# A decoder layer on one core: bank copies behind the splits, attention's output with three pairs, and two turns moved

## The chip, the cores and the metric

The kernel runs on one core of a Trainium2 chip. The metric is the device time of one execution in microseconds (us), here as the median of several runs. The engines are TensorE (PE, matmuls), VectorE (DVE), ScalarE (ACT), GpSimd (POOL) and SyncE (SP, which here only issues transfers).

## The reference

One layer of a hybrid decoder with 256 tokens of width 2048, all in float32. Two mixers work side by side on the normalised input: a gated linear recurrence, and attention with 16 heads of 128 in stick-breaking form. Their outputs are gated and merged, then projected; a gated feed-forward network and a gate with a per-layer input follow.

```python
h = rmsnorm(x, g_mix)
x_r, g_r, q, k, v, gate_r, gate_a = split(h @ w_in)
y_r = (gelu(g_r) * rg_lru(conv1d(x_r))) @ w_rnn_out            # "ro"
o   = stick_breaking_attention(head_rmsnorm(q), head_rmsnorm(k), v)   # "qk", "v"
y_a = o @ w_attn_out                                            # "ao"
x   = x + (sigmoid(gate_r) * y_r + sigmoid(gate_a) * y_a) @ w_o # "wo"
g, u = split(rmsnorm(x, g_ffn) @ w_ffn_gu)                      # "gu"
x   = x + (silu(g) * u) @ w_ffn_down                            # "dn"
x   = x + sigmoid(rmsnorm(x, g_ple) @ w_ple_gate) * (p @ w_ple_proj)  # "pg"
```

The names behind the lines are those that the kernel gives to its stages.

## The kernel before

**Three products for one.** Every matmul operand is a float32 number, held as a high part and the low rest, both in a rounded type (fp32r). A product of two is the sum of three matmuls, each 128 x 128 by 128 x 512: high by high (L657), high by low (L658), low by high (L659), in `prod`. Each weight chunk of 128 x 1024 is therefore *split* before use: ACT copies it to the high part (L374), DVE subtracts that from the weight to get the low part (L375).

**Fewer products by sums.** Most stages are computed in groups (`group`), each of 256 tokens by 1024 columns of output, in a scheme with seven products of blocks where the plain way has eight. For some *pairs* of 128-row steps of the weights, sums of weight blocks are formed (DVE L296, and a few by accumulating transfers that POOL issues, L334), and sums of the activations (`half_sums`). A group's list of *slots* names the order: whole numbers are plain steps (four products each), "11", "21", "22", "T1" to "T4" and ("S", i, p) are steps on sums. Pairs 0, 1 make the first part; ("S", i, 2) is a third pair, ("S", i, 3) a fourth. Lists with three pairs are `FIRST3` and `EVEN3`, 61 products; with four pairs `EVEN4`, 60 products. `FOUR` names the stages with four.

**Banks.** A group collects its products in PSUM banks named "B", "5", "2", "3", "4" and "8". When the partial sums "11", "T1", "T2", "T3" are complete, ACT copies the bank to SBUF (the *bank copies*, `actv(t, ps, AF.Copy)`, L460 in the profile); after T3, DVE makes two differences of the copies. The results then are four *joins*, a bank plus a copy, on DVE (L454).

**What is issued when.** The instructions of one engine run in their order in its queue. A scheduler sets this order at build, from the order of the program and estimated times. `tc.issue_after(ins)` puts what is issued inside it behind the instruction `ins` on its engine. Weights are streamed by `Stream`: it loads, sums and splits up to four chunks ahead of the matmul that asks for one, and remembers its last splits in `hi_ins` and `lo_ins`. Work that can wait is put on a list with a due time (`later_on`), and issued by `run_todo` at the slots of the next group once its time has come, each behind the last splits (`behind_splits`). The four joins are due at `JOINS_AT`, 0, 1.3, 2.7 and 4.0 us into the next group. While such work is left on the list, the turned rows (transposes, `next_mix`) that the next stage needs are held back.

**Attention.** The heads are worked in eight pairs `hp` between the blocks of matmuls for the last Q and K columns and for the gate: `step` is called before every slot of those blocks, and each slot has a list of attention steps: `att_t` (transposes of a head pair's rows, PE L1021), `att_z` (scores), `att_e` (masks and exponents) and `att_o` (the product with V). `TURN_AT` gives the slot of `att_t`, `ATT_FROM` and `ATT_AT` those of the others. From slot 60 on, the sums of attention's output for the stage "ao" are made (`parts_sums`). A slot holds four products, twelve matmuls.

**Around the change.** The order of stages is: ... gate blocks with attention, ao (two groups), wo (two), the feed-forward network (gu, dn), pg (two). `whole` computes a group and lists its joins. After each ao group, every result is joined, multiplied by its gate and added to the other mixer's result (`join`, due at 2.7 + 1.36 i); these rows are then turned for wo.

Of the kernel before, what the change touches and what calls it, by code (L numbers as in the profile page):

```python
# [10 lines left out]
AF = mybir.ActivationFunctionType  # L11
ALU = mybir.AluOpType
# [22 lines left out]
FIRST3 = ["11", A1, 6, "T1", A2, 7, "T2", "21", "22", A3, "T3", 8, A4, 9, "T4", 10, 11, 12, 13, 14, 15]  # L35
EVEN3 = ["11", A1, 6, "T1", A2, 7, "21", 8, "T2", 9, "22", A3, 10, "T3", 11, A4, 12, "T4", 13, 14, 15]
# [3 lines left out]
TWELVE = [("S", 1, 0), ("S", 1, 1), 4, ("S", 2, 0), 5, ("S", 2, 1), 6, ("S", 3, 0), 7, ("S", 3, 1), 8, ("S", 4, 0), 9,  # L40
          ("S", 4, 1), 10, 11]
TWO = (0, 1)
FOUR = ("gu", "v", "ro", "qk", "ao")
LAST_GROUP = ("pg", 1)
W_BUFS = 4
RAW_AHEAD = 12.0
# [37 lines left out]

ATT_AT = (2, 7, 11)
ATT_FROM = (-1, 6, 14, 21, 29, 36, 43, 51)
TURN_AT = (None, None, 8, 12, 25, 30, 42, 49)


def rg_k_tiles(j):  # L90
# [77 lines left out]
def tail():  # L168


    def wide(name, w, slots, c=0):
        return [(name, g, w, c + 8 * g, c + 8 * g + 4, slots[g]) for g in range(2)]

    def blocks(*cs):
        return [("blk", b, None, c, None, None) for c, b in cs]

    def gu(*gs):
        return [("gu", g, "gu", 4 * g, 44 + 4 * g, EVEN4 if g else FIRST3) for g in gs]

    def dn(q):  # L180
        k, p = FQ0[q], FQ0[q] // 2
        slots = [x + k if isinstance(x, int) else (*x[:2], x[2] + p) if isinstance(x, tuple) else x
                 for x in (EVEN3 if FQ[q] == 16 else TWELVE)]
        return wide(f"dn{q}", "dn", [slots] * 2)

    x = [("x", 0), ("x", 1)]
    return (wide("ro", "ro", [LONG] * 2) + wide("v", "in", [EVEN4] * 2, C_V)
            + [("qk", b, "in", C_Q + 4 * b, C_K + 4 * b, EVEN4) for b in range(2)]
            + blocks(*[(c, b) for b in (2, 3) for c in (C_Q, C_K)], *[(C_GTA, b) for b in range(4)])
            + wide("ao", "ao", [EVEN4] * 2) + wide("wo", "wo", [FIRST3, EVEN3]) + gu(0, 1, 2, 3) + dn(0) + gu(4, 5, 6, 7) + dn(1)  # L190
            + gu(8, 9, 10) + dn(2)
            + wide("pg", "pg", [FIRST3[:-4] + x + FIRST3[-4:]] * 2))

# [233 lines left out]
def tile_hybrid_block(ctx: ExitStack, tc: tile.TileContext, xT: bass.AP, x: bass.AP, pT: bass.AP,  # L427
# [25 lines left out]
    def tt(o, a, b, op):  # L453
        nc.vector.tensor_tensor(o, a, b, op)  # L454
# [4 lines left out]
    def actv(o, i, f, **kw):  # L459
        nc.scalar.activation(o, i, f, **kw)  # L460
# [176 lines left out]

    pend, todo = [], []

    def later_on(at, f, first=True):  # L640

        todo.append((at, f, first))

    def run_todo(t):
        due = [x for x in todo if x[0] <= t]
        todo[:] = [x for x in todo if x[0] > t]
        for _, f, _ in due:
            with behind_splits():
                f()

    def tok(pairs, k, t):
# [69 lines left out]
    def group(at, pairs, sums, after=None, also=()):  # L721

        name, g = at
        slots = [x for n, y, _, _, _, sl in HEAD + TAIL if (n, y) == at for x in sl
                 if isinstance(x, int) or is_sum(x)]  # L730
        turned_at = TURNED_AT["twelve" if len(slots) == len(TWELVE) else
                              "first" if slots[2] == 6 and slots[8] == "22" else "even"]
        seq = [(n, q, 0, 512) for n, x in enumerate(slots) for q in products(x, pairs_of(name)[:2])]
        if at == LAST_GROUP:
            k = len(slots) - 4
            rest = [q for q in seq if q[0] >= k]
            seq = [q for q in seq if q[0] < k] + [q for b in "243" for q in rest if q[1][0] == b]
            seq += [(n, (b + f, *q), e, e + 256) for e, f in ((0, "a"), (256, "b")) for n, (b, *q), _, _ in rest
                    if b == "8"]
        first, last = {}, {}  # L740
        for i, (_, (b, y, _, _), e, _) in enumerate(seq):
            first.setdefault(b, i)
            last[b, e] = i
            if y in ("11", "T1", "T2", "T3"):
                last[y] = i
        banks, tile_, got = {}, {}, {}
        begin = [0.0]
        for x in slots:
            begin.append(begin[-1] + 0.68 * len(products(x)))
        turns = list(turned_at)  # L750
        for i, (n, (b, y, p, c), e0, e1) in enumerate(seq):
            if n not in got:
                if n in also:
                    also[n]()
                run_todo(begin[n])
                if pend and turns and n >= turns[0] and not any(x[2] for x in todo):
                    turns.pop(0)
                    with tc.issue_after(mm_.ins):
                        pend.pop(0)()
                got[n] = S_.take(("tok", name, g, slots[n]))  # L760
            if b not in banks:
                banks[b] = psum()
            ps = banks[b]
            if p is None:
                o = tok(pairs, *y)
            else:
                o = {"11": tok(pairs, 2 * p, 0), "21": tok(pairs, 2 * p + 1, 0), "22": sums[p][3],
                     "T1": sums[p][0], "T2": sums[p][1], "T3": sums[p][2],
                     "T4": tok(pairs, 2 * p + 1, 1)}[y]
            _, _, hi, lo, w0 = got[n].columns(c)  # L770
            s = slice(w0 + e0, w0 + e1)
            mm_ = prod(ps[:, e0:e1], o, hi[:, s], lo[:, s], i == first[b], i in (last[b, e0], last.get(y)),
                 b == "B")
            if y in ("11", "T1", "T2", "T3") and i == last[y]:
                t = tile_[y] = tl("T")
                actv(t, ps, AF.Copy)
                if y == "T3":
                    tt(tile_["T2"], tile_["T1"], tile_["T2"], ALU.subtract)
                    tt(tile_["T1"], tile_["T1"], t, ALU.subtract)
                    if after is not None:  # L780
                        after(tile_)
        tile_["ends"] = [banks[b] for b in ("8a", "8b") if b in banks]
        return [banks[b] for b in "2438"], tile_

# [104 lines left out]
    @contextmanager  # L889
    def behind_splits():  # L890
        with tc.issue_after(S_.hi_ins.ins), tc.issue_after(S_.lo_ins.ins):
            yield
# [52 lines left out]
        else:  # L945
            pend_gtr = pss

    def whole(at, pairs, sums, also=()):

        qs_, t = group(at, pairs, sums, None, also)  # L950
        cs = [t[y] for y in ("11", "T3", "T2", "T1")]
        for a, c, q in zip(JOINS_AT, cs, qs_):
            later_on(a, (lambda c, q: lambda: tt(c, q, c, ALU.add))(c, q))
        return cs

    def parts_sums(pairs, sums, p):
        h = tl("T")
        hi, lo = parts(pairs[p])
        tt(pair(h), f32(hi), f32(lo), ALU.add)
        sums[p] = half_sums(h)  # L960
# [150 lines left out]
            at.setdefault(ATT_FROM[hp] + f, []).append(((att_z, att_e, att_o)[d], hp))  # L1111
    osum = {}
    for i, p in enumerate(pairs_of("ao")):
        at.setdefault(60 + i, []).append((lambda p: parts_sums(ost, osum, p), p))
    slot = [0]

    def step():
# [42 lines left out]
        return run  # L1160

    for g in range(2):
        for i, o in enumerate(whole(("ao", g), ost, osum)):
            def join(o=o, c=gta[2 * g + i // 2][i % 2], m=mix_r[2 * g + i // 2][i % 2]):
                tt(c, o, c, ALU.mult)
                tt(c, c, m, ALU.add)

            later_on(2.7 + 1.36 * i, join)
        pend.extend(next_mix(p) for p in range(4 * g, 4 * g + 4))

    x1 = [[None] * 4 for _ in range(2)]
# [72 lines left out]
    def gu(g):  # L1244
        also = {13: lambda: token_scales(0, rs1)} if g == 0 else {}
        c11, c21, c12, c22 = whole(("gu", g), hg, hsum, also)
        def gated(c, s_, t):
            def run():
                actv(s_, s_, AF.Silu, scale=rs1[:, t:t + 1])
                stt(c, c, rs1[:, t:t + 1], s_, ALU.mult, ALU.mult)  # L1250
            return run

        later_on(5.4, gated(c12, c11, 0))
        later_on(8.1, gated(c22, c21, 1))

        def turn(f):
            def run():
                ps = psum()
                for e in range(2):
                    for t, a in enumerate((c12, c22)):  # L1260
                        c = (2 * f + e) * P
                        o = e * 256 + t * P
                        nc.tensor.transpose(ps[:, o:o + P], a[:, c:c + P], ident)  # L1263
                p = 2 * g + f
                if p in summed:
                    h = tl("T")
                    actv(h, ps, AF.Copy)
                    acts[p] = split(h, "A")
                    asum[p] = half_sums(h)
                else:  # L1270
                    acts[p] = split(ps, "A")
            return run

        pend.extend(turn(f) for f in range(2))
# [120 lines left out]
```

## Time and profile before

| | us |
|---|---|
| median of 3 runs | 1856.26 |
| lowest and highest | 1856.01, 1857.22 |
| the profiled execution | 1855.46 |
| its span in the trace | 1853.8 |

The page gives one profiled execution: the busy time of each engine, the chain of work that ended last, and groups of instructions by line. An engine's busy time, set beside the span, says how much room it has; whether another engine's work matters is told by the waits on the engine that has none. Line numbers are those of the kernel before. Some matmul records can be missing, and the ends of matmuls are modelled: two matmuls that follow each other overlap in the rows.

### The profile page before, as it was taken

To read this page: it belongs to the slowest core of one execution; us is meant where nothing else is said; L and a number is where in the kernel's file an instruction comes from. 1 tells how busy PE (TensorE), PEld (TensorE's weight loads), DVE (VectorE), ACT (ScalarE), POOL (GpSimd) and SP (SyncE) were. 2 spreads that over 40 slices of the span, in tenths; PEclk is the share of its full clock that TensorE was granted. 3 is DMA by queue.
4 is the path that set the end of the run, shared out by engine and by line. 5 is a ranking of instruction groups with operands and counts; after the bars stand their busy time and mean duration, and the time that the engine had idled before them with its cause. 6 is when DMAs were issued, how large, how long until landed. Compare 5 with 4: busy or idle time off the path is not lost.

```text
span 1853.8 us, 24812 instructions
## 1 busy us (share of the span) xinstructions
PE 1839.0 (99%) x8849; PEld 1546.0 (83%) x8849; DVE 1542.4 (83%) x1954; ACT 1275.8 (69%) x1710; POOL 133.1 (7%) x160
## 2 busy tenths in 40 slices
PE   9999999999999999999999999999999999999998
PEld 7899889888888888888877888888888888888787
DVE  7688888677899977667899889888799988898886
ACT  7687888775566767776665687665576655676675
POOL 0000000011011100000110001100111101111000
PEclk9999999999999999999999999999999999999999
DMA  8555555588788854446988788887888878887774
GB/s 296 175 177 187 184 197 198 197 251 259 240 252 238 255 174 159 151 157 219 257 234 241 223 256 240 246 246 246 254 261 253 234 235 251 251 251 235 210 242 133
DMA packets 123964, 415.42 MB, mean 224 GB/s; under 512 B 13888, under 2 KB 14528, under 8 KB 123840
## 3 DMA queue, kind: packets, MB, share of 16 engines
q1 hardware_dynamic: 101808, 359.82, 54.8%
q0 software_dynamic: 21888, 54.01, 17.2%
q8 instruction: 69, 1.13, 0.2%
q14 instruction: 55, 0.45, 0.1%
q10 hardware_dynamic: 144, 0.01, 0.0%
HBM read 411.69 MB, written 2.10 MB: 223 GB/s over the span
## 4 chain that ended last, share of the span: by engine, by line
PE 97%; DVE 2%; ACT 1%; issue 0%; DMA 0%; SPq 0%; DVEq 0%; ACTq 0%
PE ps L657 26%; PE ps L659 26%; PE ps L658 26%; PE ps L576 9%; PE ps L580 5%; PE ps L559 1%; PE ps L560 1%; PE ps L558 1%; DVE wlo L375 1%; DVE H L454 1%; PE ps L1263 1%; PE ps L1208 0%; PE ps L1021 0%; DMA H<-in_x_dram 0%; DVE Q L454 0%
## 5 line engine op out<-in xcount | busy, mean ns | idle before, releaser
L658 PE MATMUL ps<-wlo,Q 128*128 128x512 f32 x2173 | 846.7, 390 | 0.5 <-DVE wlo L375 0.5
L659 PE MATMUL ps<-whi,Q 128*128 128x512 f32 x2173 | 843.2, 389 | 2.6 <-DVE Q L454 2.6
L657 PE MATMUL ps<-whi,Q 128*128 128x512 f32 x2173 | 752.3, 392 | 4.0 <-ACT whi L374 2.2
L375 DVE TENSOR_TENSOR wlo<-w,whi 128x1024 fp32r<-128x1024 f32 (+2 forms) x474 | 570.5, 1208 | 163.4 <-ACT whi L374 159.1
L374 ACT ACTIVATE whi<-w 128x1024 fp32r<-128x1024 f32 (+2 forms) x474 | 493.8, 1048 | 216.9 <-PE ps L659 166.3
L374 ACT ACTIVATE whi<-Q 128x1024 fp32r<-128x1024 f32 (+1 forms) x385 | 384.8, 1005 | 212.4 <-PE ps L659 177.9
L375 DVE TENSOR_TENSOR wlo<-Q,whi 128x1024 fp32r<-128x1024 f32 (+1 forms) x385 | 441.5, 1155 | 61.8 <-ACT whi L374 58.0
L657 PEld LDWEIGHTS ps<-whi,Q 128*128 128x128 f32 x2173 | 407.5, 188 | 89.2 <-ACT whi L374 3.3
L659 PEld LDWEIGHTS ps<-whi,Q 128*128 128x128 f32 x2173 | 408.0, 188 | 87.2 <-DVE Q L454 2.8
L658 PEld LDWEIGHTS ps<-wlo,Q 128*128 128x128 f32 x2173 | 408.3, 188 | 83.7 <-DVE wlo L375 1.5
L334 POOL DMA_DIRECT2D Q<-in_w_dram x152 | 130.6, 866 | 1669.9 <-PE ps L659 623.1
L576 PE MATMUL ps<-Q,whi 128*128 128x512 f32 x704 | 170.7, 392 | 0.0
L576 PEld LDWEIGHTS ps<-Q,whi 128*128 128x128 f32 x704 | 128.8, 188 | 24.5
L296 DVE TENSOR_TENSOR Q<-Q,Q 128x512 f32<-128x512 f32 (+1 forms) x152 | 130.6, 877 | 15.1 <-DMA Q<-in_w_dram 14.7
L460 ACT ACTIVATE H<-ps 128x512 f32<-128x512 f32 (+1 forms) x179 | 94.2, 540 | 61.1 <-PE ps L659 51.0
L454 DVE TENSOR_TENSOR H<-H,H 128x512 f32<-128x512 f32 (+1 forms) x216 | 121.0, 571 | 4.9 <-ACT H L460 4.3
L454 DVE TENSOR_TENSOR H<-ps,H 128x512 f32<-128x512 f32 (+1 forms) x162 | 97.2, 610 | 9.5 <-PE ps L659 5.1
L580 PEld LDWEIGHTS ps<-Q,wlo 128*128 128x128 f32 x704 | 90.4, 191 | 3.5
L580 PE MATMUL ps<-Q,wlo 128*128 128x256 f32 x704 | 91.5, 283 | 0.0
L460 ACT ACTIVATE Q<-H 128x512 fp32r<-128x512 f32 x71 | 43.8, 626 | 37.5 <-DVE H L454 36.9
L460 ACT ACT_TABLE_LOAD x52 | 66.7, 1283 | 3.1 <-DVE Q L454 2.2
L454 DVE TENSOR_TENSOR Q<-H,Q 128x512 fp32r<-128x512 f32 (+1 forms) x79 | 53.9, 688 | 3.0 <-ACT Q L460 2.9
(125 smaller groups left out, 898.6 us busy)
## 6 DMA issues: line engine op xcount, KB each, us to landing
w<-in_w_dram SPq DMA_DIRECT2D x449, 512.0 KB, 4.3
Q<-in_w_dram SPq DMA_DIRECT2D x206, 512.0 KB, 6.0
Q<-in_w_dram POOLq DMA_DIRECT2D x54, 512.0 KB, 7.0
Q<-in_w_dram POOLq DMA_DIRECT2D x98, 256.0 KB, 5.1
w<-in_w_dram SPq DMA_DIRECT2D x16, 448.0 KB, 3.2
H<-in_x_dram SPq DMA_DIRECT2D x8, 256.0 KB, 6.3
H<-in_xT_dram SPq DMA_DIRECT2D x7, 256.0 KB, 5.7
out_dram<-H SPq DMA_DIRECT2D x7, 256.0 KB, 2.5
```

The source lines that it names most:

```text
L296: add = lambda o, a, b: self.nc.vector.tensor_tensor(o, a, b, ALU.add)
L334: self.nc.gpsimd.dma_start(t[:, c:], src[:, a:a + 1024 - c], accum_op=ALU.add)
L374: self.hi_ins = self.nc.scalar.activation(h[:, q], t[:, q], AF.Copy)
L375: self.lo_ins = self.nc.vector.tensor_tensor(l[:, q], t[:, q], h[:, q].bitcast(F32), ALU.subtract)
L454: nc.vector.tensor_tensor(o, a, b, op)
L460: nc.scalar.activation(o, i, f, **kw)
L558: nc.tensor.matmul(o, wt[0], xh, start=start, stop=False)
L576: nc.tensor.matmul(pss[e], wt[0], rhs(xs, k), start=(k == 0), stop=(k == n - 1))
L580: nc.tensor.matmul(pss[e][:, :256], wt[1], rhs(xs, k)[:, :256], start=False, stop=False)
L657: nc.tensor.matmul(ps, x[0], wh, start=start, stop=False, skip_group_check=goes_on)
L658: nc.tensor.matmul(ps, x[0], wl, start=False, stop=False, skip_group_check=goes_on)
L659: return nc.tensor.matmul(ps, x[1], wh, start=False, stop=stop, skip_group_check=goes_on)
```

## The change

There are four parts.

- In `group`, the bank copies on ACT are issued behind the latest high split, and the two differences after T3, and what a stage hangs on them (`after`), behind the latest low split.
- Stage "ao" leaves `FOUR`, and its two groups use `EVEN3` in place of `EVEN4`. The sums for its three pairs are made in slots 61 to 63; before, those for four pairs in slots 60 to 63.
- In "ao", `whole(..., tied=False)` makes the four joins due at once, at 0, and `join`'s gate operations at 1.36 i in place of 2.7 + 1.36 i. Neither is put behind the splits.
- `TURN_AT` moves the turn of head pair 2 (heads 4 and 5) from slot 8 to slot 10, and that of pair 4 from 25 to 26.

```diff
-FOUR = ("gu", "v", "ro", "qk", "ao")
+FOUR = ("gu", "v", "ro", "qk")
...
-TURN_AT = (None, None, 8, 12, 25, 30, 42, 49)
+TURN_AT = (None, None, 10, 12, 26, 30, 42, 49)
...
-            + wide("ao", "ao", [EVEN4] * 2) + wide("wo", "wo", [FIRST3, EVEN3]) + ...
+            + wide("ao", "ao", [EVEN3] * 2) + wide("wo", "wo", [FIRST3, EVEN3]) + ...
...
-    def later_on(at, f, first=True):
+    def later_on(at, f, first=True, tied=True):
...
-        todo.append((at, f, first))
+        todo.append((at, f, first, tied))
...
-        for _, f, _ in due:
-            with behind_splits():
+        for _, f, _, tied in due:
+            with behind_splits() if tied else nullcontext():
                 f()
...
                 t = tile_[y] = tl("T")
-                actv(t, ps, AF.Copy)
+                with tc.issue_after(S_.hi_ins.ins):
+                    actv(t, ps, AF.Copy)
                 if y == "T3":
-                    tt(tile_["T2"], tile_["T1"], tile_["T2"], ALU.subtract)
-                    tt(tile_["T1"], tile_["T1"], t, ALU.subtract)
-                    if after is not None:
-                        after(tile_)
+                    with tc.issue_after(S_.lo_ins.ins):
+                        tt(tile_["T2"], tile_["T1"], tile_["T2"], ALU.subtract)
+                        tt(tile_["T1"], tile_["T1"], t, ALU.subtract)
+                        if after is not None:
+                            after(tile_)
...
-    def whole(at, pairs, sums, also=()):
+    def whole(at, pairs, sums, also=(), tied=True):
...
-            later_on(a, (lambda c, q: lambda: tt(c, q, c, ALU.add))(c, q))
+            later_on(a if tied else 0.0, (lambda c, q: lambda: tt(c, q, c, ALU.add))(c, q), True, tied)
...
-        at.setdefault(60 + i, []).append((lambda p: parts_sums(ost, osum, p), p))
+        at.setdefault(61 + i, []).append((lambda p: parts_sums(ost, osum, p), p))
...
-        for i, o in enumerate(whole(("ao", g), ost, osum)):
+        for i, o in enumerate(whole(("ao", g), ost, osum, tied=False)):
...
-            later_on(2.7 + 1.36 * i, join)
+            later_on(1.36 * i, join, True, False)
```

More of the change, by code (lines that the diff above doesn't have):

```diff
@@ L189, in tail @@
             + blocks(*[(c, b) for b in (2, 3) for c in (C_Q, C_K)], *[(C_GTA, b) for b in range(4)])
-            + wide("ao", "ao", [EVEN4] * 2) + wide("wo", "wo", [FIRST3, EVEN3]) + gu(0, 1, 2, 3) + dn(0) + gu(4, 5, 6, 7) + dn(1)
+            + wide("ao", "ao", [EVEN3] * 2) + wide("wo", "wo", [FIRST3, EVEN3]) + gu(0, 1, 2, 3) + dn(0) + gu(4, 5, 6, 7) + dn(1)
             + gu(8, 9, 10) + dn(2)
```

## The prediction

> **What bounds the kernel now.** I read the head of the page first, then who waited on TensorE, then the table by stretches, and only then single moments. The page:
>
> ```profile
> span 1853.8 us, 24812 instructions
> PE 1839.0 (99%) x8849; PEld 1546.0 (83%) x8849; DVE 1542.4 (83%) x1954; ACT 1275.8 (69%) x1710; POOL 133.1 (7%) x160
> PE 97%; DVE 2%; ACT 1%; issue 0%; DMA 0%; SPq 0%; DVEq 0%; ACTq 0%
> ```
>
> TensorE (PE) is busy for 1839.0 of 1853.8 us, and the chain that ended last runs through it for 97%. Work taken from VectorE (DVE), ScalarE (ACT) or the DMA queues is therefore worth only what PE waits for them. All of these waits (engine line, waited for: us, times, longest) are:
>
> ```profile
> PE ps L659 <- DVE Q L454: 2.6, 1, 2.6
> PE ps L657 <- ACT whi L374: 2.2, 3, 1.1
> PE ps L495 <- DVE H L492: 1.6, 1, 1.6
> PE ps L657 <- DVE Q L454: 1.2, 1, 1.2
> PE ps L657 <- DVE H L454: 0.5, 1, 0.5
> PE ps L658 <- DVE wlo L375: 0.5, 1, 0.5
> ```
>
> That is 8.6 us; the 1.6 of L495 lies at the kernel's start, which the change does not touch, and 7.0 are left. The table by stretches (us; busy time and count of PE, PEld, DVE, ACT, POOL; granted clock, DMA share, GB/s) says where:
>
> ```profile
> 700.00:960.00 260.00, 260.00 (x1270) 219.09 (x1269) 200.90 (x279) 183.89 (x282) 10.33 (x12) 1.00 0.61 195
> 960.00:1000.00 40.00, 35.13 (x156) 26.98 (x155) 39.23 (x48) 22.74 (x27) 3.44 (x4) 1.00 0.75 204
> 1000.00:1750.00 750.00, 750.00 (x3374) 620.44 (x3373) 657.05 (x760) 490.72 (x591) 78.97 (x92) 1.00 0.81 246
> 1750.00:1760.00 10.00, 8.94 (x39) 6.84 (x38) 7.55 (x10) 4.62 (x6) 2.59 (x3) 1.00 0.69 137
> 1760.00:1848.00 88.00, 87.69 (x406) 72.91 (x404) 69.75 (x84) 61.00 (x84) 4.33 (x5) 1.00 0.61 192
> ```
>
> Three places hold nearly all of it: the 1.2 us on L454, near 696 (attention's heads 4 and 5, turned), 4.87 in 960 to 1000 (the start of wo0, the output projection's first group), 1.06 in 1750 to 1760 (the start of pg0). Between them PE never waits, at full clock, so an edit there can win nothing and can only open a new wait.
>
> PE's own price comes from the chain:
>
> ```profile
> 71.41 3.65 PE ps L576 x16
> ```
>
> 3.65 / 16 = 0.228 us from one 512-column matmul to the next.
>
> **What a stop costs.** First the turned heads:
>
> ```profile
> 694.67 1.04 PE L1021 MATMUL ps<-ident,H 128*128 128x128 f32 x8
> 696.15 1.01 DVE L454 TENSOR_TENSOR Q<-Q,ps 128x512 f32<-128x512 f32 x2
> 696.88 0.50 PE L657 MATMUL ps<-whi,Q 128*128 128x512 f32 x1 [1.17 <-DVE Q L454]
> ```
>
> A matmul row lasts 0.39 but the next one normally starts after 0.228, so a stop loses its idle time and that overlap of 0.16; and the first matmul after it takes 0.50 instead of 0.39, 0.11 more. A stop costs its idle plus about 0.27: here 1.17 + 0.27 = 1.44.
>
> **Heads 4 and 5 turned two steps later (-1.44).** Now eight transposes, the previous heads' mask work and a new block's first matmul meet in slot 8. That matmul needs a PSUM bank, and the bank handed to it is the one that the DVE subtraction at 696.15 still reads. With the turn in slot 10, the block of K begins in slot 8 on banks that the score step left earlier, and by slot 10, two slots of twelve matmuls (2.7 us each) later, the bank in question is free. The turned heads' score step comes in slot 16, six slots later, so nothing else becomes late; the same move from 25 to 26 meets no wait now and keeps three slots of room. I take the whole 1.44; at worst the stop moves and nothing is won.
>
> **The start of wo0 (-6.6).** These rows, of ACT, DVE and PE, follow each other:
>
> ```profile
> 964.72 1.83 DVE L296 TENSOR_TENSOR Q<-Q,Q 128x1024 f32<-128x1024 f32 x2
> 966.68 0.60 ACT L460 ACTIVATE H<-ps 128x512 f32<-128x512 f32 x1 [4.90 <-PE ps L659]
> 967.17 1.06 ACT L374 ACTIVATE whi<-Q 128x1024 fp32r<-128x1024 f32 x1
> 967.31 0.69 DVE L454 TENSOR_TENSOR H<-H,H 128x512 f32<-128x512 f32 x1 [0.77 <-ACT H L460]
> 967.92 0.69 DVE L296 TENSOR_TENSOR Q<-Q,Q 128x512 f32<-128x512 f32 x1
> 968.70 1.06 ACT L374 ACTIVATE whi<-Q 128x1024 fp32r<-128x1024 f32 x1 [0.47 <-DVE Q L296]
> 969.81 1.08 PE L657 MATMUL ps<-whi,Q 128*128 128x512 f32 x2 [1.13 <-ACT whi L374]
> 973.12 1.22 DVE L375 TENSOR_TENSOR wlo<-w,whi 128x1024 fp32r<-128x1024 f32 x1
> 973.26 0.50 PE L657 MATMUL ps<-whi,Q 128*128 128x512 f32 x1 [0.53 <-DVE H L454]
> 974.25 0.69 DVE L454 TENSOR_TENSOR H<-ps,H 128x512 f32<-128x512 f32 x1
> 980.12 1.23 DVE L375 TENSOR_TENSOR wlo<-Q,whi 128x1024 fp32r<-128x1024 f32 x1
> 981.41 0.50 PE L658 MATMUL ps<-wlo,Q 128*128 128x512 f32 x1 [0.47 <-DVE wlo L375]
> 991.15 1.30 DVE L454 TENSOR_TENSOR Q<-ps,Q 128x512 fp32r<-128x512 f32 x2
> 991.90 1.20 PE L659 MATMUL ps<-whi,Q 128*128 128x512 f32 x4 [2.60 <-DVE Q L454]
> ```
>
> Four stops: 1.13 + 0.53 + 0.47 + 2.60 = 4.73, plus 4 x 0.27 = 5.8. The row at 969.81 holds two matmuls over 1.08, so their starts are 0.58 apart instead of 0.23: 0.35 more, and 0.11 for the second; a like small stop near 983 brings the sum to 6.6.
>
> A count agrees. The same 40 us held, among 156 instructions of PE, 16 transposes:
>
> ```profile
> L1151 PE MATMUL ps<-ident,Q 128*128 128x128 f32 x16 | 2.5, 276 | 0.0
> ```
>
> A transpose takes PE 0.11 ((1.04 - 0.27) / 7 from the row at 694.67): 140 x 0.228 + 16 x 0.11 = 33.7, which leaves 6.3.
>
> The first two stops come from the order on ACT. It idles 4.90 us in front of the copy of bank "11", while the sum that it could split was ready when the first L296 of 964.72 ended, near 965.95. DVE then waits 0.77 for the same copy before it can make the next sum. Behind the split of plain slot 7 the copy lets the T1 split start 1.2 us sooner, and the sum of 967.92 follows directly at 966.55, done by 967.2; its split ends at 968.3, when PE wants it (968.5). The bank of 973.26 is freed by a join that ran late; untied joins begin as soon as their banks end.
>
> The last two stops come from DVE, 39.23 of 40 us busy: 4 joins and 8 gate operations lie among the splits as late as 988, and the mixed rows are turned and subtracted, at 991.15, just when PE needs them. I walk the new order. DVE's pitch is 0.60 for a join or half-width sum and 1.13 for a split or full-width sum (973.12, 974.25 and on). From the first join to the low split of T2 stand 12 x 0.60, four low splits and one wide sum (5 x 1.13) and one sum of 0.60: 13.5 us. The first bank ends nine matmuls (2.05 us) before attention's output ends, so that split ends 11.5 to 12.2 us after that end. PE reaches it after 48 matmuls (10.9), eight transposes (0.9) and one more matmul (0.2): 12.0. So DVE is what is late next, by nothing or by 0.2; I book one stop of 0.4. Later low splits come every 1.13 where PE needs one per 1.37, so it does not grow, and the turned rows' sums end four us before their transposes.
>
> **Three pairs in attention's output (+1.4).** Each of two groups computes 61 products instead of 60, three matmuls each: 6 x 0.228 = 1.37 on PE, which has no cover. What it saves per group, one and a half wide splits on each of ACT and DVE and two sums, about 2.9 us of DVE, is worth nothing inside the stage (no waits in 700 to 960); it is what lets DVE reach wo0 without arrears, and it is in the walk.
>
> The Trainium skill, TensorE: Matmul & The Clock Gate, section Back-to-back issue gap, gives about 131 ns sustained for a 512-wide matmul; an estimate by it would be 0.8 us instead of 1.37. The trace's 228 ns decides here.
>
> **The start of pg0 (-1.6).**
>
> ```profile
> 1750.69 1.73 POOL L334 DMA_DIRECT2D Q<-in_w_dram  x2 [28.39 <-DVE Q L296]
> 1752.43 0.60 ACT L460 ACTIVATE H<-ps 128x512 f32<-128x512 f32 x1 [4.92 <-PE ps L659]
> 1755.49 0.50 PE L657 MATMUL ps<-whi,Q 128*128 128x512 f32 x1 [0.61 <-ACT whi L374]
> 1756.44 0.96 PE L657 MATMUL ps<-whi,Q 128*128 128x512 f32 x3 [0.45 <-ACT whi L374]
> 1760.67 0.40 PE L657 MATMUL ps<-whi,Q 128*128 128x512 f32 x1
> ```
>
> The same copy, the same cure: 0.61 + 0.45 + 2 x 0.27 = 1.6. ACT stood idle 4.92 us ahead of it, and the splits can go into that. The page of the profile gives for the transfers of the first row's kind (KB each, us from issue to landing):
>
> ```profile
> Q<-in_w_dram POOLq DMA_DIRECT2D x98, 256.0 KB, 5.1
> ```
>
> The one for T2's sum, issued at 1750.69, is what is late next: 1750.69 + 5.1, a sum of 1.13 and a split of 1.06 give 1758.0, and PE's first matmul on T2, now at 1760.67, moves up to 1759.1. The stop is gone, with a microsecond to spare.
>
> **Costed at nothing.** Bank copies in the other groups: each now waits behind one more high split, 1.06. PE writes the same bank again after 18 matmuls, 4.1 us, in the tightest list, so a copy of 0.60 behind a split of 1.06 stays 2.4 us clear. T1 and T2 subtractions and the x1 additions wait behind one low split, 1.22; they feed additions that are needed only at the next stage. On SyncE's queue the loads of x1 move ahead of some wo0 weights as their slots come free earlier, but the weight load in front of them waits longer still. POOL issues four accumulating loads fewer. After the last matmul nothing changes.
>
> **Sum.** -1.44 - 6.6 - 1.6 = -9.65; +1.37 for six matmuls; +0.4 for DVE: -7.9. The profiled execution took 1855.46 (its span and 1.66 around it), so 1847.6; the median of the runs, 1856.26, lies 0.80 above it, and I set the forecast at 1856.26 - 7.9 = 1848.4. About 0.2%, 3.7 us, is what a measurement of this kernel tells from no change.
>
> **Rivals.**
> - DVE remains the limit of wo0. It has 39.23 us of work where PE, without stops, spends 33.7; taking off the 2.9 saved and the 0.77 it idled leaves 1.9 over, and 4.8 if the saving is lost earlier to waits. Then 1848.4 - 0.4 + 1.9 to 4.8 = 1849.9 to 1852.8. For it: the margins above are a few tenths. Against: splits and sums for later slots need not all be done by 1000. Chance 0.18.
> - The order hardly changes where it matters: the copies go late but a sum or a join keeps the splits waiting as before, and only the turn and part of the rest is won: between 1853 and 1856.26 + 1.4 = 1857.7. Against: ACT's 4.90 and 4.92 us of idle time are named as waits for that bank. Chance 0.10.
> - Slower: the copies of all 29 groups go behind splits that themselves wait for a sum or a load, and the bank is not free when PE comes back. It decides once such a split starts more than 2.4 us after the bank is done. A stop then costs 0.27 and its wait; two in each group with no wait to speak of are 58 x 0.27 = 15.7, and the time 1864. For it: every bank copy now inherits the split's wait. Against: ACT is at 69% and mostly splits ahead of need. Chance 0.06.
>
> **How the numbers follow.** All three stalls go: 0.66, from 1847.4 (no stop left, a small gain unseen) to 1849.7. With DVE's case 0.84 lies below 1852.8. The range 1847.0 to 1853.0 takes both, and leaves out the third and fourth. Faster by over 0.2% is below 1852.55: the first case and nearly all of the second, 0.82. Within it: the third with a rest, 0.11. Slower: 0.07.
>
> **What would show it.** In the changed profile: no idle time near 696 and near 1755; in the wo0 stage the high split of T1 directly behind its sum, with the "11" copy after slot 7's split; all joins within four us of attention's output's end; six more matmuls. DVE near 100% for ten us there with a PE wait on L375 or L454 above one us would be the second case. PE waits on ACT L460 or DVE L454 spread over groups that have none now would make me wrong.

## The result and the profile after

Over 20 runs each the changed kernel takes 1853.24 us (1851.61 to 1854.43), the kernel before 1856.48 (1855.23 to 1857.96). The ratio is 0.9982, 95% interval 0.9975 to 0.9989: 3.2 us faster, where 7.9 were forecast. It lies just above the range, and just inside the 0.2% that I had called no change. The profiled execution took 1853.38 with a span of 1851.7.

Line numbers behind 640 are up by one from the kernel before (the three matmuls are now L658 to L660), those behind 780 by up to three. The waits of PE after (us, times, longest):

```profile
PE ps L658 <- DVE H L454: 2.1, 1, 2.1
PE ps L495 <- DVE H L492: 1.6, 1, 1.6
PE ps L658 <- ACT whi L374: 1.4, 2, 1.0
PE ps L659 <- DVE wlo L375: 0.5, 1, 0.5
```

The waits of the kernel before, but that of L495 at the start, are gone from their places. Those on this list stand elsewhere: 2.1 and 0.5 us in pg0, 1.0 of L374 in gu0 and its other 0.4 at the kernel's start. The table by stretches shows the stages:

```profile
690.00:700.00 10.00, 10.00 (x53) 8.52 (x53) 8.36 (x12) 5.25 (x7) 0.00 (x0) 1.00 0.63 206
960.00:1000.00 40.00, 40.00 (x185) 32.88 (x184) 37.97 (x46) 23.07 (x28) 2.98 (x4) 1.00 0.78 231
1040.00:1060.00 20.00, 18.97 (x84) 15.36 (x83) 18.09 (x27) 8.63 (x11) 2.59 (x3) 1.00 0.73 200
1740.00:1765.00 25.00, 22.33 (x94) 17.70 (x93) 22.30 (x28) 17.66 (x27) 3.44 (x4) 0.93 0.71 166
```

The turned heads and wo0 are as forecast, without a stop (156 instructions of PE in 960 to 1000 before, 185 now). But gu0 stops where it did not before, and pg0 stops longer. The last row's clock of 0.93 was 1.00 before. PE's rows there:

```profile
1745.68 0.50 PE L659 MATMUL ps<-wlo,Q 128*128 128x512 f32 x1 [0.55 <-DVE wlo L375]
...
1750.12 0.39 PE L660 MATMUL ps<-whi,Q 128*128 128x512 f32 x1
1752.63 0.50 PE L658 MATMUL ps<-whi,Q 128*128 128x512 f32 x1 [2.12 <-DVE H L454]
1752.97 0.40 PE L659 MATMUL ps<-wlo,Q 128*128 128x512 f32 x1
1753.20 0.49 PE L660 MATMUL ps<-whi,Q 128*128 128x512 f32 x1
1753.49 2.33 PE L658 MATMUL ps<-whi,Q 128*128 128x512 f32 x5
```

After the stop, five matmuls take 2.33 us. Taking off the last one's 0.63, four steps of 0.43 are left, where 0.228 is usual: PE runs at about half its clock for some 3 us. The granted clock is 0.50 from 1753.36 to 1756.77, which is 3.41 us.

How one stage stands is told below by its *lost time*: the sum, over its matmuls, of what the distance from one start to the next exceeds the usual one for that shape, from the trace of one execution of each kernel, good to about 0.1. Between 0.1 and 0.5 in a stage is the usual rest around transposes.

Each ratio is to runs of the kernel before on the same chip, whose median was 1856.5 to 1856.8.

| kernel | median us | ratio to before, 95% interval | turned heads | wo0 | gu0 | pg0 |
|---|---|---|---|---|---|---|
| before | 1856.5 | | 1.46 | 6.98 | 0.35 | 1.95 |
| after | 1853.24 | 0.9982 (0.9975 to 0.9989) | 0.12 | 0.52 | 1.66 | 5.16 |
| e2_no_lo | 1847.23 | 0.9949 (0.9936 to 0.9961) | 0.12 | 0.44 | 0.36 | 0.35 |
| e2b_no_copies | 1855.83 | 0.9996 (0.9988 to 1.0005) | 0.12 | 0.52 | 6.33 | 3.30 |
| e3_part1_only | 1857.34 | 1.0005 (0.9997 to 1.0014) | 1.40 | 4.87 | 1.67 | 3.57 |
| e4_turn_only | 1855.92 | 0.9996 (0.9987 to 1.0005) | 0.12 | 8.61 | 0.36 | 1.95 |
| e1_no_order | 1848.47 | 0.9956 (0.9944 to 0.9969) | 0.12 | 0.44 | 0.36 | 1.95 |
| e6_lo_not_dn | 1848.95 | 0.9960 (0.9947 to 0.9972) | 0.12 | 0.51 | 1.66 | 0.35 |
| e7_earlier_split | 1846.70 | 0.9947 (0.9934 to 0.9959) | no waits of PE behind the kernel's start, in any stage | | | |
| e8_four_pairs | 1852.51 | 0.9977 (0.9967 to 0.9987) | 0.12 | 6.71 | 0.36 | 0.35 |
| e9_late_joins | 1848.15 | 0.9957 (0.9944 to 0.9971) | 0.12 | 1.72 | 0.36 | 0.35 |

### The profile page after: what moved, and what is told of

The parts are those of the page before. It is cut to its first block, busy times and chain, and to the rows that moved or that the text cites. A ratio compares the mean times of both kernels' runs of the same rounds, so it can differ in the third digit from the quotient of the medians.

```text
span 1851.7 us, 24795 instructions
## 1 busy us (share of the span) xinstructions
PE 1840.0 (99%) x8855; PEld 1547.8 (84%) x8855; DVE 1535.5 (83%) x1940; ACT 1269.9 (69%) x1705; POOL 129.5 (7%) x156
## 4 chain that ended last, share of the span: by engine, by line
PE 96%; DVE 2%; ACT 1%; DMA 1%; issue 0%; SPq 0%; ACTq 0%
PE ps L658 26%; PE ps L659 26%; PE ps L660 26%; PE ps L576 9%; PE ps L580 5%; PE ps L559 1%; PE ps L560 1%; PE ps L558 1%; DVE wlo L375 1%; DVE H L454 1%; DMA w<-in_w_dram 1%; PE ps L1266 1%; PE ps L1024 0%; ACT whi L374 0%; PE ps L1211 0%
## 5 line engine op out<-in xcount | busy, mean ns | idle before, releaser
L660 PE MATMUL ps<-whi,Q 128*128 128x512 f32 x2175 | 845.4, 389 | 0.0
L658 PE MATMUL ps<-whi,Q 128*128 128x512 f32 x2175 | 752.4, 392 | 3.5 <-DVE H L454 2.1
L374 ACT ACTIVATE whi<-w 128x1024 fp32r<-128x1024 f32 (+2 forms) x478 | 497.6, 1047 | 215.5 <-PE ps L660 167.3
L374 ACT ACTIVATE whi<-Q 128x1024 fp32r<-128x1024 f32 (+1 forms) x377 | 376.5, 1004 | 227.9 <-PE ps L660 182.1
L375 DVE TENSOR_TENSOR wlo<-Q,whi 128x1024 fp32r<-128x1024 f32 (+1 forms) x377 | 431.3, 1153 | 66.7 <-ACT whi L374 64.1
L658 PEld LDWEIGHTS ps<-whi,Q 128*128 128x128 f32 x2175 | 408.6, 188 | 88.0 <-DVE H L454 2.5
L660 PEld LDWEIGHTS ps<-whi,Q 128*128 128x128 f32 x2175 | 408.6, 188 | 84.3
L334 POOL DMA_DIRECT2D Q<-in_w_dram x148 | 126.8, 863 | 1671.6 <-PE ps L660 670.3
L454 DVE TENSOR_TENSOR H<-H,H 128x512 f32<-128x512 f32 (+2 forms) x214 | 119.3, 570 | 2.2 <-ACT H L460 1.0
L454 DVE TENSOR_TENSOR H<-ps,H 128x512 f32<-128x512 f32 (+1 forms) x162 | 96.6, 606 | 11.5 <-PE ps L660 6.9
L454 DVE TENSOR_TENSOR Q<-H,Q 128x512 fp32r<-128x512 f32 (+1 forms) x78 | 52.9, 683 | 2.1 <-ACT Q L460 2.1
```

The lines of the kernel that those rows point to most:

```text
L334: self.nc.gpsimd.dma_start(t[:, c:], src[:, a:a + 1024 - c], accum_op=ALU.add)
L374: self.hi_ins = self.nc.scalar.activation(h[:, q], t[:, q], AF.Copy)
L375: self.lo_ins = self.nc.vector.tensor_tensor(l[:, q], t[:, q], h[:, q].bitcast(F32), ALU.subtract)
L658: nc.tensor.matmul(ps, x[0], wh, start=start, stop=False, skip_group_check=goes_on)
L660: return nc.tensor.matmul(ps, x[1], wh, start=False, stop=stop, skip_group_check=goes_on)
```

## The experiments

**Where the loss comes from: the low-split part, the copies, or the lead.** The first part of the change has two halves: the bank copies on ACT behind the high split, and the DVE work after T3 (two differences, and in wo and dn the additions to x1) behind the low split. Each was undone by itself, the first part was put alone on the kernel before, and so were the turns.

```diff
e2_no_lo, against after
-                    with tc.issue_after(S_.lo_ins.ins):
-                        tt(tile_["T2"], tile_["T1"], tile_["T2"], ALU.subtract)
+                    tt(tile_["T2"], tile_["T1"], tile_["T2"], ALU.subtract)
...
e2b_no_copies, against after
-                with tc.issue_after(S_.hi_ins.ins):
-                    actv(t, ps, AF.Copy)
+                actv(t, ps, AF.Copy)
...
e3_part1_only, against before
+                with tc.issue_after(S_.hi_ins.ins):
+                    actv(t, ps, AF.Copy)
...
+                    with tc.issue_after(S_.lo_ins.ins):
+                        tt(tile_["T2"], tile_["T1"], tile_["T2"], ALU.subtract)
...
e4_turn_only, against before
-TURN_AT = (None, None, 8, 12, 25, 30, 42, 49)
+TURN_AT = (None, None, 10, 12, 26, 30, 42, 49)
```

> The changed kernel, with the T1 and T2 differences and the x1 additions after T3 issued as before, not behind the latest low split; all else of the change stays. Theory A (these DVE instructions, moved, make the turned rows of pg0 late, and that is where the gain went): the stops of pg0 fall from about 5.2 us of lost time to between 0.4 and 2, the clock stays at 1.00 there, the time is 1848.5 to 1850. Theory B (the bank copies behind the high split do it): no change, 1853. Theory C (PE, 5 us earlier after wo0, catches up with ACT and DVE at pg0 whatever their order): no change, 1853.

1847.23 us: theory A, and 1.3 us below the range that it gave. The only wait of PE left in the whole kernel is the one at its start:

```profile
PE ps L495 <- DVE H L492: 1.6, 1, 1.6
```

and the stretch of pg0 is full, at full clock:

```profile
1740.00:1765.00 25.00, 25.00 (x118) 20.69 (x117) 24.59 (x31) 19.87 (x34) 3.44 (x4) 1.00 0.67 140
```

B and C fall: the copies are as in the changed kernel, and PE comes to pg0 still earlier.

> The changed kernel, with the bank copies on ACT issued as before, not behind the latest high split; the differences and x1 additions stay behind the low split. Theory A: pg0 keeps its stops or gets 1.6 us more, and wo0's first stops come back in part: 1853 to 1857. Theory B: pg0's stops go, 1850 or below. Theory C: 1853 to 1856.

1855.83, inside A's range, but inside C's too, and the stages are only in part as A had them: pg0 keeps stops (3.30), wo0's first stops do not come back (0.52), and gu0 loses 6.33, which no theory had. The clock has a share in that. PE stops five times between 1053.4 and 1060.7, for 0.95, 0.30, 0.68, 0.78 and 0.45 us, and then the stretch reads:

```profile
1060.00:1064.00 4.00, 3.55 (x9) 2.67 (x9) 4.00 (x5) 0.63 (x1) 0.85 (x1) 0.57 0.45 62
```

B falls a second time here, since pg0's stops stay when the copies are back at their old place.

> The kernel before, with the first part of the change alone: bank copies behind the high split, differences and x1 additions behind the low split. Theory A: pg0 loses 3 us more than in the kernel before, wo0 loses 2 to 3 less: 1856 to 1858. Theory B: the same. Theory C: PE is not early here, so pg0's stops go: 1852 to 1853.

1857.34 beside 1856.76 for the kernel before on the same chip, not told apart. The stages are as A had them, though pg0 loses less than A's 3 us: wo0 loses 2.1 less, and gu0 and pg0 lose 1.3 and 1.6 more, though PE is not early here. C falls a second time; B, which expected the same as A, is not tested by this run.

> The kernel before, with the two turns moved to slots 10 and 26 alone. All theories: the stop near 696 goes, 1.4 us, nothing else changes: 1855.0. If a later block pays it back: 1856.4.

The stop of the turned heads goes (1.46 to 0.12), yet the median falls by 0.8 and is not told apart. In the profiled execution wo0 takes it back, 8.61 for 6.98, by the clock. After wo0's stop of 2.35 us the stretch reads:

```profile
992.00:996.00 4.00, 4.00 (x12) 3.14 (x11) 4.00 (x7) 2.11 (x2) 0.00 (x0) 0.60 0.90 327
```

In the kernel before, after its stop of 2.60, it reads:

```profile
992.00:996.00 4.00, 4.00 (x18) 3.29 (x19) 4.00 (x7) 2.01 (x2) 0.00 (x0) 1.00 0.87 351
```

**What the low split does to the work behind it.** DVE's rows after, ahead of pg0, in the feed-forward's last group, dn2:

```profile
1731.07 0.69 DVE L454 TENSOR_TENSOR Q<-H,Q 128x512 fp32r<-128x512 f32 x1 [0.67 <-ACT Q L460]
1732.02 1.23 DVE L375 TENSOR_TENSOR wlo<-w,whi 128x1024 fp32r<-128x1024 f32 x1 [0.26 <-ACT whi L374]
1733.16 0.68 DVE L375 TENSOR_TENSOR wlo<-Q,whi 128x512 fp32r<-128x512 f32 x1
1733.76 1.29 DVE L454 TENSOR_TENSOR H<-H,H 128x512 f32<-128x512 f32 x2
...
1739.12 1.22 DVE L375 TENSOR_TENSOR wlo<-w,whi 128x1024 fp32r<-128x1024 f32 x1
```

and ACT's, which made the last two bank copies of that group and the high part for the split at 1733.16:

```profile
1725.93 1.08 ACT L460 ACTIVATE H<-ps 128x512 f32<-128x512 f32 x2
...
1732.24 0.64 ACT L374 ACTIVATE whi<-Q 128x512 fp32r<-128x512 f32 x1 [0.26 <-PE ps L660]
```

The copies were ready at 1727.0, and the first difference runs at 1733.76, 6.8 us later, right behind a low split whose high half had waited for PE. DVE had other work ahead in its queue for most of that time, but it was not full: it idles 0.67 and 0.26 in these rows. The split tied to is up to four chunks ahead of PE, and its buffer comes free only when PE has used an older chunk. Here its high half could begin only at 1732.24, 5.2 us after the copies. In e2_no_lo the copies end at 1723.40 (ACT), and the two differences follow within 0.1 (DVE; the row holds one 128x128 instruction and then both):

```profile
1722.32 1.08 ACT L460 ACTIVATE H<-ps 128x512 f32<-128x512 f32 x2
1723.27 1.61 DVE L454 TENSOR_TENSOR H<-H,H 128x128 f32<-128x128 f32 x3
```

After the change the differences and the additions to x1 then come just when DVE has to make the sums of the turned rows for pg0. ACT stands idle for 4.67 us until it can copy one of these sums:

```profile
1741.17 0.63 ACT L460 ACTIVATE Q<-H 128x512 fp32r<-128x512 f32 x1 [4.67 <-DVE H L454]
1744.41 2.36 DVE L375 TENSOR_TENSOR wlo<-Q,whi 128x1024 fp32r<-128x1024 f32 x2 [0.46 <-ACT whi L374]
```

In e2_no_lo the wait at the same instruction is 0.70:

```profile
1735.10 0.63 ACT L460 ACTIVATE Q<-H 128x512 fp32r<-128x512 f32 x1 [0.70 <-DVE H L454]
1737.72 1.22 DVE L375 TENSOR_TENSOR wlo<-Q,whi 128x1024 fp32r<-128x1024 f32 x1
```

So ACT is 6.1 us and DVE 6.7 us later than in e2_no_lo, while PE, by the lost time up to 1740, is only about 2 us later. The first of the splits at 1744.41 ends PE's stop of 0.55, and from it on DVE works without a gap until PE's long stop ends. The last part of the chain:

```profile
1746.68 1.22 DVE wlo L375
1747.90 1.74 DVE Q L296 x2
1749.64 0.60 DVE Q L454
1750.24 0.60 DVE Q L296
1750.84 1.14 DVE wlo L375
1751.98 0.61 DVE H L454
1752.59 0.04 issue
1752.63 0.50 PE ps L658
```

These are a low split, the sums, T1's low split, and behind that dn2's first join (H L454), which frees the bank that PE waits for at 1752.63.

Two runs test this reading: the tie loosened in the dn groups alone, and the same tie to an earlier low split.

```diff
e6_lo_not_dn, against after
-                    with tc.issue_after(S_.lo_ins.ins):
+                    with tc.issue_after(S_.lo_ins.ins) if name[:2] != "dn" else nullcontext():
e7_earlier_split, against after (los: all low splits in their order)
-                    with tc.issue_after(S_.lo_ins.ins):
+                    with tc.issue_after(S_.los[-5].ins):
```

> The changed kernel, with the differences and x1 additions after T3 issued as before in the groups of the feed-forward's second half (dn) alone; in all other groups they stay behind the latest low split. If pg0's loss comes from the dn groups ahead of it: pg0's stops go and the 1.3 us at gu0 stay, 1848.3 to 1849.5. If the order of all groups adds up: 1850 or more.

1848.95: pg0's loss comes from the tie in the dn groups ahead of it. gu0's 1.3 stays, so it comes from the tie in another group; the wo groups lie just ahead of it, but no run loosens the tie in them alone.

> The changed kernel, with the differences and x1 additions issued behind the low split that lies four splits before the latest one (T3's own, which is done by then). If the harm is the wait that they inherit (the latest low split waits for PE to free a buffer): no stop at gu0 or pg0, 1846.8 to 1848. If being tied to any split, and the order that the scheduler makes of it, is the harm: 1850 to 1853.

1846.70, the lowest median of all though not told apart from e2_no_lo, and PE without a wait behind the kernel's start. The tie as such does no harm; the place behind the latest split does. This run takes away both the wait that this split carries and the work that stands ahead of it, and does not part the two; the row at 1732.24 above shows the wait. Nor does a run part the differences from the additions to x1.

**What each other part is worth.** e1_no_order is the changed kernel with both halves of the first part undone, the two edits of e2_no_lo and e2b_no_copies together.

> The changed kernel without its first part: bank copies, differences and x1 additions are all issued as before; the three pairs, the early joins and the turns stay. If the copies' new place is what removes pg0's stops of 1.6 us: these come back, the time is 1848.5 to 1849.5, above the 1847.2 without the low-split part alone. If wo0's first stops (2.6 us) hung on the copies as I said, they come back too: 1851. If the copies' place is worth nothing: 1847.2.

1848.47: pg0's 1.95 are back and 1.24 us of the time with them, so the copies' new place is worth about that (the runs were on different chips, but none of the one kernel reaches those of the other). But wo0's first stops, which I had put down to the copies, stay away.

```diff
e8_four_pairs, against e2_no_lo
-FOUR = ("gu", "v", "ro", "qk")
+FOUR = ("gu", "v", "ro", "qk", "ao")
...
-            + wide("ao", "ao", [EVEN3] * 2) + ...
+            + wide("ao", "ao", [EVEN4] * 2) + ...
...
-        at.setdefault(61 + i, []).append(...)
+        at.setdefault(60 + i, []).append(...)
e9_late_joins, against e2_no_lo
-        for i, o in enumerate(whole(("ao", g), ost, osum, tied=False)):
+        for i, o in enumerate(whole(("ao", g), ost, osum)):
...
-            later_on(1.36 * i, join, True, False)
+            later_on(2.7 + 1.36 * i, join)
```

> The changed kernel without the low-split part and without the three pairs: attention's output in four pairs again, sums from slot 60 on; early joins, copies behind high splits and turns stay. If the early joins alone cure wo0: 1845.9, the 1847.2 less six matmuls. If DVE needs the 2.9 us that three pairs save it: wo0's stops come back by 2 to 4 us, 1848 to 1850, and more where the clock falls.

1852.51, worse than expected: wo0 loses 6.71. The stretch shows stops of 1.55, 0.45 and 0.80 us and again a fallen clock, at 0.50 for 6.83 us:

```profile
970.00:980.00 10.00, 7.24 (x19) 5.13 (x20) 10.00 (x13) 7.47 (x9) 1.71 (x2) 0.66 0.32 67
```

DVE is full, 10.00 of 10: without the three pairs it is in arrears when wo0 begins.

> The changed kernel without the low-split part, and with attention's joins and gate operations due and tied as before; the three pairs stay. If the three pairs alone cure wo0: 1847.2, no stop there. If the early joins are needed as well: wo0's stops come back by 2 to 5 us, 1849 to 1852, and more with the clock.

1848.15, between the two expectations: one stop of 0.9 is left in wo0.

```profile
PE ps L660 <- DVE Q L454: 0.9, 1, 0.9
```

So the three pairs do most for wo0, and the early joins the last 1.3 us.

**The clock and the spread of the runs.** The changed kernel's runs lie in two clusters, so three more single executions of it were profiled.

> The changed kernel itself, one more look. Its 20 runs lie in two clusters, 1851.6 to 1852.4 and 1853.1 to 1854.4. If what parts them is the clock after pg0's stop: a time in the lower cluster goes with a granted clock of 1.00 there, one in the upper with about 0.6 over some 3 us. If not: no such pairing.

It took 1852.08, and behind the stop the clock stays:

```profile
1753.00:1757.00 4.00, 4.00 (x18) 3.31 (x19) 4.00 (x5) 1.89 (x4) 0.85 (x1) 1.00 1.01 174
```

> The changed kernel, a second look, with the same two expectations as the first.

It took 1853.87:

```profile
1753.00:1757.00 4.00, 3.88 (x11) 3.14 (x12) 4.00 (x6) 1.89 (x3) 0.86 (x1) 0.65 1.01 176
```

Eighteen instructions of PE in four microseconds in the one, eleven in the other, after the same stop (2.12 and 2.08). pg0 loses 3.57 and 5.14: the clock costs 1.6.

> The changed kernel, a third look, with the same two expectations as the first.

1853.57, with the clock at 1.00 there, pg0 losing 3.54. The pairing does not hold: this run lost 0.7 more than look1 at the kernel's start and 0.8 more in gu1, together the 1.5 us between the two. The clock makes part of the spread, not all.

## Why the prediction was right or wrong, point by point

- **What bounds the kernel, and the price of a stop:** right. PE bounds it; the three places were the ones that could go, and in e2_no_lo they all went, with nothing new.
- **The turned heads, -1.44:** right in the trace, 1.46 to 0.12. By itself it could not be told from no change in the median.
- **wo0, -6.6:** right in size (6.98 to 0.52), and the residual of 0.4 was nearly nothing. Half of its reason was wrong, so the size is in part luck: the first part takes 2.1 off the stage when it is made alone (e3_part1_only), but with three pairs and early joins the first stops go without it (e1_no_order). The DVE time that the three pairs save, which I had only for the last two stops, carries most of wo0, and without it first stops come back (e8_four_pairs).
- **Six matmuls, +1.37:** PE has six more (8855 for 8849), but their time is not measured apart. Without the three pairs wo0's stops come back and hide it.
- **pg0, -1.6:** right for the copies (1.24 in the median, 1.6 in the trace), and lost in the change as a whole, where pg0 gets 3.2 worse.
- **The step that failed** is in "Costed at nothing": "T1 and T2 subtractions and the x1 additions wait behind one low split, 1.22". I priced the split at its duration, not at its wait and the work ahead of it, and took what stands behind it to have time until the next stage. The split tied to is the latest one issued, it hangs on PE through its buffer, and ahead of pg0 the work behind it came 6.8 us after its copies and made that next stage late. It cost 1.3 at gu0 and, with the clock, up to 4.8 at pg0; 6.0 us between the medians of the changed kernel and e2_no_lo. My slower rival had the mechanism, a place inherited with the split's wait, but I had looked for it on ACT's copies and PSUM banks alone and given it 0.06.
- **The median:** e2_no_lo, which is the forecast's sum without the failed step, gains 9.5 where I had 7.9. Between the two profiled executions, neither with a fall of the clock while PE works, the gain is 9.0 (1855.46 to 1846.49), of which 0.4 lies at the kernel's start, where executions vary, and 0.4 is the DVE stop that I had booked and that did not come. Medians may gain more, since the clock may fall behind a stop that is then gone; how often it falls in the kernel before was not measured, and where the rest comes from stays open.

## What to carry to other kernels

Work that is put behind another instruction inherits that instruction's wait, not just its duration: before tying something to "the latest" prefetch, ask what that prefetch waits for and what stands ahead of it, and tie to one that is done by then. Here the tie to a split four places earlier took a loss of 6 us away. When an engine off the critical path is nearly full ahead of a stage, taking work from it there can be worth more than the work that PE gets for it: e2_no_lo is 5.3 us faster than e8_four_pairs, with six matmuls more.

## What the runs showed of the hardware

PE's granted clock fell to 0.50 for 3.41 us (0.57 to 0.65 in the rows above, which are 4 us long) after stops as short as 2.1 to 2.4 us (the changed kernel, look2, e4_turn_only). It fell for twice that, 6.83 us, in e8_four_pairs behind a stop of 1.55 followed by 0.45, and for 3.41 us at gu0 of e2b_no_copies in a row of five stops of which none is longer than 0.95 us, 3.2 us in all within 7.3. The same stop as in the changed kernel did not do it in look1 and look3, nor did one of 2.60 in the kernel before. A fall of 3.41 us costs 1.6 us, by pg0 in look1 and look2. What decides whether a stop brings one on is not shown.

The Trainium skill, TensorE: Matmul & The Clock Gate, section HAM oscillation, names PE idle gaps over about 3.4 us as the condition. These runs show it with shorter ones.
